# Reordering the first stage of a hybrid attention step: blank products, an earlier weight transfer, and 256-token products that lag by three

## The chip, the cores and the metric

One NeuronCore of a Trainium2 chip runs the whole program. The metric is the time of one execution on the device, in microseconds (us); before the change its median over three runs is 698.73 us (698.7 to 698.9). The engines are named as in the profile: PE is the matrix engine (PEld its weight loads), DVE the vector engine, ACT the scalar engine, POOL the GpSimd engine, SP the engine that issues most of the transfers. Each engine works through its own instructions in the order in which they stand, and semaphores tie the engines together.

## The reference: what is computed

One layer of a diffusion backbone on 128 context tokens and 1024 latent tokens, 1024 channels, all in float32:

```python
shift, scale, gate = split(silu(cond) @ w_mod + b_mod, 3)      # cond: c_ctx for context, c for latent
h = rmsnorm(x, norm_gain) * (1 + scale) + shift
q_a, k_a, v_a, g_a, q_b, k_b, v_b, g_b = split(h @ w_in)       # two head groups, 8 heads of 64 each
# rms norm of q and k per head, rotary positions on latent tokens,
# group A: attention to all keys, group B: band of +-128 keys with a sink; both also to the context keys
x = x + gate * (concat(o_a * silu(g_a), o_b * silu(g_b)) @ w_out)
```

The outputs are the new x of both token sets and the context keys and values. Only the part up to `g_a = h @ w_in[:, g_a]` matters here, that is the modulation, the norm and the first projection.

## The kernel before

Tokens lie in nine tiles of 128: tile 0 is the context, tiles 1 to 8 the latent tokens. Channels lie in eight blocks of 128, counted by k or j. The first stage (lines 430 to 563) does this for every tile: load it (`load_x`, L387), square and sum it on ACT (`squares`, L392), turn the mean square into a factor on POOL (L394, L396), multiply the tile by it on DVE (`scaled`, L399), turn it on PE in eight 128x128 transposes (`turned_tile`, L409) and copy the result from the two banks to `xT`, one half on ACT and one on DVE (`keep`, L413).

Beside it, for each channel block j, 1 MB of modulation weights `wm[j]` is loaded (`load_wm`, L334, three buffers). Eight small PE products give the modulation rows (`modulate_rows`, L363), a copy and two PE transposes bring them into columns (`modulate`, L374 to L380), and `modulated` (L424 to L428) makes the modulated block `h` as a high part `h0` (ACT) and a low part `h1` (`hf` on DVE, then a difference on POOL). The weights of the gate projection arrive as eight blocks `rawga` of 256 KB (`W_GA.load`, L229, three buffers) and are split likewise into `whiga` (ACT, L241) and `wloga` (DVE, L243).

The loop `for j in range(1, KT + 2)` (L498) is what the rest of the text calls steps. Step j does the gate products of block j-1 for the first 512 tokens: four output chunks `pg_f` ("big", `first_gates`), each with three products of 128x512 (high by high, high by low, low by high: L270, L271, L266). In the same step stand the modulation of block j, which the next step's products need, and the turning of one more tile: tile 5 in step 1, tile 6 in step 2, tiles 7, 8, 0 in steps 3, 4, 5 (`rest`). The squares of tile 7, 8 or 0 are taken one step before it is turned. Twelve products of 128x256 for tokens 512 to 767 (`pg_s`, "small", `next_gates`) close each step from step 2 on, for block j-2. `warm(n)` issues n products of a zero tile ("blank products", L447) whose result nobody reads.

What sets the order: `in_order` (L100) ties the instructions of every engine to the order in which the Python code writes them, so no scheduler moves anything. All transfers of this stage but one are issued by SP, into one queue; a transfer is issued when its buffer is free, and those behind it wait for it.

Of the kernel before, what the change touches and what calls it, by code (L numbers as in the profile page):

```python
# [36 lines left out]
LAG = 3  # L37
LEAD = 4
# [22 lines left out]
WARM = (12, 4)  # L61
# [53 lines left out]
def hybrid_step(ctx, tc, x_prompt, x_sample, cache_k_a, cache_v_a, cache_k_b, cache_v_b,  # L115
# [31 lines left out]
    mm_tags = ["BAAB"]  # L147
# [173 lines left out]
    with tc.tile_pool(name="st", bufs=2, side="right") as st:  # L321
# [27 lines left out]
        def conditions():  # L349

            nc.vector.tensor_copy(colt, pcol)
            nc.vector.tensor_copy(sil32[:, :, 0:2], sil2)
            nc.vector.tensor_scalar(bsc1, colt[:, 32:40], 1.0, None, op0=ALU.add)
            nc.vector.tensor_copy(ident_r, ident)
            nc.gpsimd.tensor_scalar(diag, ident[0:4, 0:4], -1.0, None, op0=ALU.mult)
# [14 lines left out]
        def modulate(j):  # L370
            pm = pmod.pop(j)[:, 256:512]
            for s in range(2):
                cs = slice(P * s, P * s + P)
                nc.tensor.transpose(pm[:, cs], mrows[j][:, cs], ident)  # L374
            m4 = st.tile([P, 2, 2], F32, tag="m4", name=f"m4_{j}")
            nc.vector.tensor_reduce(m4, pm.rearrange("p (s g c) -> p s c g", s=2, c=32)[:, :, 0:2, :], axis=AX.X,
                                    op=ALU.add)
            nc.vector.tensor_scalar(a_mod[:, j, :], m4[:, 0], bsc1[:, j : j + 1], colt[:, 16 + j : 17 + j],
                                    op0=ALU.add, op1=ALU.mult)
            nc.vector.tensor_scalar(b_col[:, j, :], m4[:, 1], colt[:, 24 + j : 25 + j], None, op0=ALU.add)  # L380

        xn, rx, px = {}, {}, {}
        xT = st.tile([P, KT, TOK], F32, name="xT", bufs=1)

        def load_x(t):
            xn[t] = st.tile([P, D], F32, tag="xn", name=f"xn{t}", bufs=4)
            nc.sync.dma_start(xn[t], x_tile[t])  # L387

        def squares(t):
            sq = st.tile([P, D], BF16, tag="sq", name=f"sq{t}", bufs=1)  # L390
            ss = st.tile([P, 1], F32, tag="ss", name=f"ss{t}")
            nc.scalar.activation(sq, xn[t], AF.Square, accum_out=ss)  # L392
            ms = st.tile([P, 1], F32, tag="ms", name=f"msx{t}")
            nc.gpsimd.tensor_scalar(ms, ss, 1.0 / D, EPS, op0=ALU.mult, op1=ALU.add)  # L394
            rx[t] = st.tile([P, 1], F32, tag="rs", name=f"rsx{t}", bufs=4)
            nc.gpsimd.tensor_tensor(rx[t], ms, mhalf[:, 0:1], op=ALU.pow)  # L396
# [4 lines left out]
        def turned_tile(t, tags, between=None):  # L401

            for c in range(2):
                if c and between:
                    between()
                px[t, c] = bank(tags[c], f"px{t}_{c}")
                for i in range(4):
                    k = 4 * c + i
                    nc.tensor.transpose(px[t, c][:, P * i : P * i + P], xn[t][:, P * k : P * k + P], ident)  # L409

        def keep(t, c, copy):
            at = slice(P * place(t), P * place(t) + P)
            copy(xT[:, 4 * c : 4 * c + 4, at], px.pop((t, c)).rearrange("p (k n) -> p k n", n=P))  # L413
# [16 lines left out]
        for t in (1, 2, 3, 4):  # L430
            load_x(t)
        load_wm(0)
        W_GA.load()
        load_wm(1)
        load_x(5)
        load_x(6)
        W_GA.load()
        load_wm(2)
        W_GA.load()
        load_x(7)  # L440
        load_x(8)
# [24 lines left out]
        nc.tensor.transpose(pcol, crow, ident[0:48, 0:48])  # L466
        for t in (1, 2, 3, 4):
# [3 lines left out]
        for t, tags in ((1, "AB"), (2, "AB"), (3, "CC")):  # L471
            scaled(t)
            if t == 2:
                conditions()
            if t == 3:
                modulate_rows(0, 0)
            turned_tile(t, tags)
            if t > 1:
                for c in range(2):
                    keep(t - 1, c, copies[c])  # L480
        scaled(4)
        modulate_rows(0, 1)
        keep(3, 0, copies[0])
        W_GA.split(nc.gpsimd)
        turned_tile(4, "AB", lambda: modulate(0))
        keep(4, 0, copies[0])
        modulated(0, 1, 4, 0)
        keep(3, 1, copies[1])
        keep(4, 1, copies[1])
        load_wm(3)  # L490
        load_x(0)
        squares(5)
        warm(WARM[1])
        big = [bank("AABB"[ch], f"pg0_{ch}_f") for ch in range(4)]
# [3 lines left out]
        for j in range(1, KT + 2):  # L498
            big_on, small_on = j <= KT, 2 <= j
# [4 lines left out]
            if big_on:  # L504
# [4 lines left out]
            if j == 2:  # L509
                turned_tile(6, "CC")  # L510
                for c in range(2):
                    keep(6, c, copies[c])
                small = [bank("C", f"pg0_{ch}_s") for ch in (0, 2)]
                for k in range(2):
                    modulated(k, 5, 2, 0)
            if j < KT:
                modulate_rows(j)
                if j + 3 < KT:
                    load_wm(j + 3)
            if j == 1:  # L520
                scaled(5)
                squares(6)
# [4 lines left out]
            if big_on:  # L527
                first_gates(0, j - 1, 1)
                first_gates(1, j - 1, 1)
                first_gates(2, j - 1, 1 if j == KT else None)  # L530
            if j < KT:
                modulate(j)
                if j == 1:
                    W_GA.split()
                modulated(j, 1, 4, 0)
                if j == 1:
                    scaled(6)
            if big_on:
                first_gates(3, j - 1)
            if j == 1:  # L540
                turned_tile(5, "DE")
                for c in range(2):
                    keep(5, c, copies[c])
# [6 lines left out]
            for ch in range(4):  # L550
                if small_on:
                    next_gates(ch, j - 2)
# [912 lines left out]
```

## Time and profile before

| what | value |
|---|---|
| median of three runs | 698.73 us (698.7 to 698.9) |
| the profiled execution's own time | 698.91 us |
| its span, first to last instruction | 697.2 us |
| granted PE clock, mean | 0.999 |
| PE busy | 689.9 us, 99% of the span |
| first real product of step 1 | 14.90 us |
| steps 2, 3 and 4 begin on PE | 20.24, 27.22 and 33.83 us |

Times inside the span count from its first instruction. A row of the timeline gives the start, the length, the engine, the line and operation, output and inputs, shape, how many equal ones were merged, and in brackets the idle time before it with the engine that ended it. The table of stretches gives for each stretch the busy time of each engine with its number of instructions, the granted PE clock, the mean busy share of the 16 DMA engines and what they moved in GB/s. A row of the chain of waits is start, length and what ran or was waited for.

### The profile page before, as it was taken

How to read it: one execution, taken by the hardware profiler on the slowest of the kernel's cores; microseconds unless marked ns; L12 is line 12 of the kernel's file. 1: busy time of each engine (PE TensorE's matmuls, PEld its weight loads, DVE VectorE, ACT ScalarE, POOL GpSimd, SP SyncE). 2: the span in 40 equal slices, each digit the busy share in tenths (PEclk: the TensorE clock that was granted, in tenths of full speed). 3: DMA queues.
4: the chain of work that ended last, by engine and by line, in shares of the span. 5: the costliest groups of instructions: out<-in, count | busy, mean ns of one | idle time of the engine just before them, and what ended most of it. 6: DMA issues, size and time to landing. Idle time of an engine off the chain costs nothing.

```text
span 697.2 us, 10663 instructions
## 1 busy us (share of the span) xinstructions
PE 689.9 (99%) x3537; PEld 558.6 (80%) x3537; DVE 464.3 (67%) x1010; ACT 409.9 (59%) x845; POOL 340.3 (49%) x359
## 2 busy tenths in 40 slices
PE   8999999999999999999999999999999999999997
PEld 4778988878788889987878888788788888887876
DVE  4767258968778855757777577666775775675563
ACT  6646312412423423198787887787778778877770
POOL 4547033232223420269665745565566557556751
PEclk9999999999999999999999999999999999999999
DMA  9962283359444016433122121212221221212323
GB/s 345 412 216 90 77 304 77 91 145 276 109 105 122 18 59 209 132 102 99 49 78 83 46 84 54 91 39 76 69 84 36 80 75 47 84 53 91 100 75 122
DMA packets 53336, 78.51 MB, mean 113 GB/s; under 512 B 6952, under 2 KB 25496, under 8 KB 52384
## 3 DMA queue, kind: packets, MB, share of 16 engines
q1 hardware_dynamic: 45040, 65.86, 28.6%
q10 hardware_dynamic: 8240, 11.96, 6.4%
q8 instruction: 28, 0.46, 0.3%
q14 instruction: 28, 0.23, 0.1%
HBM read 58.63 MB, written 19.18 MB: 112 GB/s over the span
## 4 chain that ended last, share of the span: by engine, by line
PE 94%; DMA 2%; ACT 2%; DVE 1%; issue 0%; SPq 0%; POOL 0%; ACTq 0%
PE po L1311 14%; PE pv L1233 7%; PE pv L1230 7%; PE st L1209 5%; PE pmx L920 5%; PE pv L1232 5%; PE st L1210 5%; PE pq L256 5%; PE pq L258 5%; PE pq L257 5%; PE st L1204 4%; PE pg L266 3%; PE pg L270 3%; PE pg L271 3%; PE pk L257 2%; PE pk L258 2%
## 5 line engine op out<-in xcount | busy, mean ns | idle before, releaser
L1220 POOL TENSOR_TENSOR pl<-pe,ph 128x512 fp32r<-128x512 f32 x130 | 168.5, 1298 | 134.2 <-DVE nm L976 65.4
L921 DVE TENSOR_REDUCE mx<-pmx 128x1 f32<-128x384 f32 x192 | 101.2, 553 | 56.1 <-PE pmx L920 54.0
L1212 ACT ACTIVATE pe<-st 128x512 f32<-128x512 f32 x146 | 86.9, 595 | 28.3 <-PE st L1210 27.7
L1216 ACT CAST ph<-pe 128x512 fp32r<-128x512 f32 x146 | 90.7, 621 | 4.8
L1230 PE MATMUL pv<-ph,v_hi 128*128 128x512 f32 x208 | 82.3, 396 | 0.1
L1233 PE MATMUL pv<-pl,v_hi 128*128 128x512 f32 x208 | 82.1, 395 | 0.2 <-DVE pl L1206 0.2
L976 DVE CUSTOM_DVE_ANT_0 sn<-sn,mask,nsink 128x512 f32<-128x512 f32 (+1 forms) x64 | 46.3, 724 | 41.9 <-PE sn L973 40.5
L181 POOL TENSOR_TENSOR rs_q<-ms_q,mhalf 128x8 f32<-128x8 f32 x18 | 34.2, 1898 | 80.8 <-DVE ms_q L179 80.8
L1311 PE MATMUL po<-wo,ogh 128*128 128x512 f32 (+1 forms) x224 | 73.4, 388 | 0.0
L920 PE MATMUL pmx<-kha,qt 128*128 128x384 f32 x192 | 60.4, 362 | 0.0
L1209 PE MATMUL st<-qt,kha 128*128 128x512 f32 x144 | 57.9, 402 | 0.0
L1232 PE MATMUL pv<-ph,v_lo 128*64 128x512 f32 x146 | 57.6, 395 | 0.0
L1210 PE MATMUL st<-qb,kla 68*128 68x512 f32 x144 | 57.3, 398 | 0.0
L1233 PEld LDWEIGHTS pv<-pl,v_hi 128*128 128x128 f32 x208 | 39.0, 188 | 17.5 <-DVE pl L1206 0.6
L962 ACT ACTIVATE pen<-sn,nm 128x512 f32<-128x512 f32 (+2 forms) x72 | 45.0, 627 | 6.0 <-DVE nm L976 2.7
L1205 ACT CAST ph<-st 128x512 fp32r<-128x512 f32 x62 | 36.4, 587 | 20.1 <-PE st L1204 18.8
L1311 PEld LDWEIGHTS po<-wo,ogh 128*128 128x128 f32 x224 | 41.0, 188 | 6.4 <-ACT ogh L1273 0.3
L1230 PEld LDWEIGHTS pv<-ph,v_hi 128*128 128x128 f32 x208 | 39.2, 189 | 7.6 <-issue 0.6
L1206 DVE TENSOR_TENSOR pl<-st,ph 128x512 fp32r<-128x512 f32 x62 | 42.5, 686 | 2.8 <-ACT ph L1205 2.3
L679 ACT CAST qo0q<-ptq 128x512 fp32r<-128x512 f32 x18 | 10.6, 587 | 57.4 <-PE ptq L676 57.4
L1311 PE MATMUL po<-wo,ogl 128*128 128x512 f32 (+1 forms) x112 | 43.6, 389 | 0.0
L920 PEld LDWEIGHTS pmx<-kha,qt 128*128 128x128 f32 x192 | 35.4, 190 | 4.5
(238 smaller groups left out, 1702.3 us busy)
## 6 DMA issues: line engine op xcount, KB each, us to landing
qt<-qd SPq DMA_DIRECT2D x36, 256.0 KB, 3.2
wm<-in_w_mod_ss_dram SPq DMA_DIRECT2D x7, 1024.0 KB, 11.1
qd<-qo0q ACTq DMA_DIRECT2D x36, 128.0 KB, 2.4
qd<-qo1q ACTq DMA_DIRECT2D x36, 128.0 KB, 2.4
sgl<-gd SPq DMA_DIRECT2D x35, 128.0 KB, 2.6
out_dram<-yt SPq DMA_DIRECT2D x17, 256.0 KB, 2.1
xn<-in_x_sample_dram SPq DMA_DIRECT2D x8, 512.0 KB, 6.1
wg<-in_w_mod_g_dram SPq DMA_DIRECT2D x4, 1024.0 KB, 8.5
```

The costliest lines, as they stand in the source:

```text
L257: nc.tensor.matmul(out, h_at(0, i, k, tok), w.lo[k], start=False, stop=False)
L920: nc.tensor.matmul(pm[:, 0:384], lhs, kha[:, g, 3 * b : 3 * b + 3, :], start=True, stop=True)
L921: nc.vector.tensor_reduce(mx[:, h, b : b + 1], pm[:, 0:384], axis=AX.X, op=ALU.max)
L1209: nc.tensor.matmul(s, kh, qtile[i], start=True, stop=False)
L1210: nc.tensor.matmul(s, kl, qbtile[i], start=False, stop=True)
L1212: nc.scalar.activation(pe, s, AF.Exp)
L1216: nc.scalar.copy(ph, pe)
L1220: nc.gpsimd.tensor_tensor(pl, pe, ph, op=ALU.subtract)
L1230: nc.tensor.matmul(pv, two, ph, start=(b == 0), stop=False)
L1232: nc.tensor.matmul(pv[0:64, :], vl, ph, start=False, stop=False)
L1233: nc.tensor.matmul(pv, two, pl, start=False, stop=last)
L1311: nc.tensor.matmul(po[n, q.start], a, wo_parts[KT * n + k][lo][:, q], start=(k == KS[0] and p == 0), stop=(k == KS[-1] and p == 2))
```

## The change

Five things move, all in the first stage.

- Blank products: sixteen become 25. Five new ones stand behind the transpose of the conditions, two before tile 2's transposes and two before tile 3's.
- The head: the four tiles' squares come first on ACT; tile 4 is scaled straight after tile 3 on DVE but for one copy; the eight modulation products of block 0 run in one go. Small preparations go from DVE to ACT and POOL, and for blocks 0 and 1 the shift column (`b_col`) goes to ACT. For tiles 1 to 6 the mean square needs no step on POOL any more: the square is scaled on ACT, and a 1025th element holds the constant.
- Transfers: the fourth modulation weights `wm3` are asked for before tiles 7, 8 and 0. Tile 6 goes behind the second gate weights.
- Steps 1 and 2: step 1 takes its products of three chunks high part first; its DVE split of the second gate weights stands ahead of the modulation's reduction; tile 6 is turned at the end of step 2 and not in its middle.
- The small products lag by three steps and not two, so that the loop has one step more; the banks of the big outputs alternate (ABAB).

On SP's queue, before (the x tiles are `xn`, the modulation weights `wm`, the gate weights `rawga`):

```order
L387 DMA xn5_190<-in_x_sample_dram 128x1024
L387 DMA xn6_192<-in_x_sample_dram 128x1024
L229 DMA rawga_1_194<-in_w_in_dram 128x512
L334 DMA wm2_196<-in_w_mod_ss_dram 128x2048
L229 DMA rawga_2_198<-in_w_in_dram 128x512
L387 DMA xn7_200<-in_x_sample_dram 128x1024
L387 DMA xn8_202<-in_x_sample_dram 128x1024
L229 DMA rawga_3_307<-in_w_in_dram 128x512
L334 DMA wm3_333<-in_w_mod_ss_dram 128x2048
```

and with the change:

```order
L392 DMA xn5_194<-in_x_sample_dram 128x1024
L230 DMA rawga_1_196<-in_w_in_dram 128x512
L392 DMA xn6_198<-in_x_sample_dram 128x1024
L335 DMA wm2_200<-in_w_mod_ss_dram 128x2048
L230 DMA rawga_2_202<-in_w_in_dram 128x512
L335 DMA wm3_204<-in_w_mod_ss_dram 128x2048
L230 DMA rawga_3_316<-in_w_in_dram 128x512
L392 DMA xn7_342<-in_x_sample_dram 128x1024
```

Up to `rawga_2` the same bytes are asked for; behind it tile 7 (`xn7`) came next, and now `wm3` and `rawga_3` stand ahead of it.

On ACT, from the cast of the third gate weights in step 2 to the first products' operand of step 3 (`sq7` is the square of tile 7, `h0_0_2` the high part of block 2 for 512 tokens, `mrows2` the copy of block 2's modulation rows), before:

```order
L241 CAST whiga_2_415<-rawga_2_198 128x512
L413 COPY xT_174<-px6_0_425 128x4x128
L424 ACTIVATE h0_1_0_132<-xT_174,b_col_150,a_mod_149 128x256 x2
L368 COPY mrows2_456<-pm2_447 128x256
L392 ACTIVATE sq7_460,ss7_461<-xn7_200 128x1024
L424 ACTIVATE h0_0_2_118<-xT_174,b_col_150,a_mod_149 128x512
```

and with the change:

```order
L242 CAST whiga_2_419<-rawga_2_202 128x512
L368 COPY mrows2_438<-pm2_429 128x256
L401 ACTIVATE sq7_445,ms7_446<-xn7_342 128x1024
L433 ACTIVATE h0_0_2_118<-xT_174,b_col_150,a_mod_149 128x512
L422 COPY xT_174<-px6_0_469 128x4x128
L433 ACTIVATE h0_1_0_132<-xT_174,b_col_150,a_mod_149 128x256 x2
```

The square of tile 7 still stands directly ahead of `h0_0_2`; tile 6's copy and the 256-token operands went behind them.

On DVE in step 1, before:

```order
L368 COPY mrows1_366<-pm1_357 128x256
L399 TENSOR_SCALAR xn5_190<-xn5_190,rsx5_342 128x1024
L376 TENSOR_REDUCE m4_1_385<-pm1_357 128x4
L378 TENSOR_SCALAR a_mod_149<-m4_1_385,bsc1_170,colt_163 128x2
L380 TENSOR_SCALAR b_col_150<-m4_1_385,colt_163 128x2
L243 TENSOR_TENSOR wloga_1_390<-rawga_1_194,whiga_1_389 128x512
```

and with the change:

```order
L368 COPY mrows1_373<-pm1_364 128x256
L408 TENSOR_SCALAR xn5_194<-xn5_194,rsx5_347 128x1024
L244 TENSOR_TENSOR wloga_1_381<-rawga_1_196,whiga_1_380 128x512
L376 TENSOR_REDUCE m4_1_391<-pm1_364 128x4
L378 TENSOR_SCALAR a_mod_149<-m4_1_391,bsc1_170,colt_163 128x2
```

The split of the second gate weights moved ahead of the reduction, and the shift column left DVE.

The diff, cut to its core:

```diff
+LEADING = (1, 2, 3, 4, 5, 6)
-WARM = (12, 4)
+WARM = (12, 5, 2, 2, 4)
...
-            nc.vector.tensor_scalar(b_col[:, j, :], m4[:, 1], colt[:, 24 + j : 25 + j], None, op0=ALU.add)
+            bias = colt[:, 24 + j : 25 + j]
+            if j < 2:
+                nc.scalar.activation(b_col[:, j, :], m4[:, 1], AF.Identity, bias=bias)
+            else:
+                nc.vector.tensor_scalar(b_col[:, j, :], m4[:, 1], bias, None, op0=ALU.add)
...
         def squares(t):
-            sq = st.tile([P, D], BF16, tag="sq", name=f"sq{t}", bufs=1)
-            ss = st.tile([P, 1], F32, tag="ss", name=f"ss{t}")
-            nc.scalar.activation(sq, xn[t], AF.Square, accum_out=ss)
-            ms = st.tile([P, 1], F32, tag="ms", name=f"msx{t}")
-            nc.gpsimd.tensor_scalar(ms, ss, 1.0 / D, EPS, op0=ALU.mult, op1=ALU.add)
+            n = D + (t in LEADING)
+            sq = st.tile([P, D + 1], BF16, tag="sq", name=f"sq{t}", bufs=1)
+            ms = st.tile([P, 1], F32, tag="ms", name=f"ms{t}")
+            nc.scalar.activation(sq[:, 0:n], xe[t][:, 0:n], AF.Square, scale=D ** -0.5, accum_out=ms)
+            if t not in LEADING:
+                nc.gpsimd.tensor_scalar(ms, ms, EPS, None, op0=ALU.add)
...
         load_wm(1)
         load_x(5)
+        W_GA.load()
         load_x(6)
-        W_GA.load()
         load_wm(2)
         W_GA.load()
-        load_x(7)
-        load_x(8)
+        load_wm(3)
...
+        scaled(1)
+        turned_tile(1, "AB")
+        scaled(2)
+        nc.vector.tensor_copy(sil32[:, :, 0:2], sil2)
+        warm(WARM[2])
+        turned_tile(2, "AB")
+        scaled(3)
+        warm(WARM[3])
+        turned_tile(3, "CC")
+        for t in (1, 2, 3):
+            keep(t, 0, copies[0])
+        keep(1, 1, copies[1])
         scaled(4)
-        modulate_rows(0, 1)
-        keep(3, 0, copies[0])
+        keep(2, 1, copies[1])
+        keep(3, 1, copies[0])
+        modulate_rows(0)
...
-        load_wm(3)
-        load_x(0)
+        load_x(7)
         squares(5)
...
+        late = {1: 8, 2: 0}
-        for j in range(1, KT + 2):
-            big_on, small_on = j <= KT, 2 <= j
+        for j in range(1, KT + 3):
+            big_on, small_on = j <= KT, 3 <= j
...
-            if j == 2:
-                turned_tile(6, "CC")
...
             if j < KT:
                 modulate_rows(j)
                 if j + 3 < KT:
                     load_wm(j + 3)
+                if j in late:
+                    load_x(late[j])
...
-            if j == 1:
-                turned_tile(5, "DE")
+            if j in (1, 2):
+                turned_tile(4 + j, ("CC", "DE")[j - 1])
...
                 if small_on:
-                    next_gates(ch, j - 2)
+                    next_gates(ch, j - 3)
```

More of the change, by code (lines that the diff above doesn't have):

```diff
@@ L146, in hybrid_step @@
     turn = {"mm": 0, "tr": 0}
[L147 removed]
+    mm_tags = ["BABA"]
     def bank(tag, name):
@@ L349, in conditions @@
         def conditions():
[L351 to L354, printed above, removed]
+            nc.scalar.copy(colt, pcol)
+            nc.gpsimd.tensor_scalar(bsc1, colt[:, 32:40], 1.0, None, op0=ALU.add)
+            nc.gpsimd.tensor_copy(ident_r, ident)
             nc.gpsimd.tensor_scalar(diag, ident[0:4, 0:4], -1.0, None, op0=ALU.mult)
@@ L403, in turned_tile, with keep @@
             for c in range(2):
-                if c and between:
-                    between()
                 px[t, c] = bank(tags[c], f"px{t}_{c}")
                 for i in range(4):
+                    if c and i == 2 and between:
+                        between()
                     k = 4 * c + i
                     nc.tensor.transpose(px[t, c][:, P * i : P * i + P], xn[t][:, P * k : P * k + P], ident)
-        def keep(t, c, copy):
+        def keep(t, c, copy, a=0, b=4):
             at = slice(P * place(t), P * place(t) + P)
-            copy(xT[:, 4 * c : 4 * c + 4, at], px.pop((t, c)).rearrange("p (k n) -> p k n", n=P))
+            copy(xT[:, 4 * c + a : 4 * c + b, at], px[t, c].rearrange("p (k n) -> p k n", n=P)[:, a:b])
         def modulated(j, t0, n, cond):
@@ L431, in hybrid_step @@
             load_x(t)
+            padded(t, nc.vector)
         load_wm(0)
@@ L503, in hybrid_step @@
                 put_gates(big[0], 0, 0, slice(0, 512))
-            if big_on:
+            if j == 1:
+                for part in (W_GA.hi, W_GA.lo):
+                    for ch in range(3):
+                        nc.tensor.matmul(big[ch], part[0][:, P * ch : P * ch + P], h_at(0, 0, 0, slice(0, 512)),
+                                         start=(part is W_GA.hi), stop=False)
+            elif big_on:
                 first_gates(0, j - 1, 0)
@@ L508, in hybrid_step @@
                     first_gates(2, j - 1, 0)
-            if j == 2:
-                turned_tile(6, "CC")
-                for c in range(2):
-                    keep(6, c, copies[c])
+            if j == 3:
                 small = [bank("C", f"pg0_{ch}_s") for ch in (0, 2)]
-                for k in range(2):
-                    modulated(k, 5, 2, 0)
             if j < KT:
@@ L519, in hybrid_step @@
                     load_wm(j + 3)
+                if j in late:
+                    load_x(late[j])
+            if j in (1, 2):
+                scaled(4 + j)
             if j == 1:
-                scaled(5)
-                squares(6)
+                W_GA.split()
             if j in rest:
@@ L529, in hybrid_step @@
                 first_gates(1, j - 1, 1)
-                first_gates(2, j - 1, 1 if j == KT else None)
+                first_gates(2, j - 1, 1 if j in (1, KT) else None)
             if j < KT:
                 modulate(j)
-                if j == 1:
-                    W_GA.split()
                 modulated(j, 1, 4, 0)
                 if j == 1:
-                    scaled(6)
+                    squares(6)
             if big_on:
                 first_gates(3, j - 1)
-            if j == 1:
-                turned_tile(5, "DE")
+            if j in (1, 2):
+                turned_tile(4 + j, ("CC", "DE")[j - 1])
                 for c in range(2):
-                    keep(5, c, copies[c])
+                    keep(4 + j, c, copies[c])
+            if j == 2:
+                for k in range(2):
+                    modulated(k, 5, 2, 0)
             if j in rest:
```

29 lines of the change are left out of this document (13 added, 16 removed).

## The prediction

> **What bounds the kernel now.** I read the page first (span, busy shares, the chain that ended last), then PE's own waits over the whole run, then the table of stretches, and then the timeline of each engine where the change acts.
>
> ```profile
> span 697.2 us, 10663 instructions
> PE 689.9 (99%) x3537; PEld 558.6 (80%) x3537; DVE 464.3 (67%) x1010; ACT 409.9 (59%) x845; POOL 340.3 (49%) x359
> PE 94%; DMA 2%; ACT 2%; DVE 1%; issue 0%; SPq 0%; POOL 0%; ACTq 0%
> ...
> PE px L409 <- DVE xn L399: 1.2, 2, 0.8
> PE idle L447 <- DVE mhalf L170: 1.0, 1, 1.0
> PE pm L363 <- DMA wm<-in_w_mod_ss_dram: 0.2, 1, 0.2
> PE sn L972 <- ACT pen L962: 0.2, 1, 0.2
> ```
>
> PE bounds the whole run, and its waits, all in the head but for single ones of 0.2 us, make some 3 us. So two things follow. There is little to win: the change reorders the first 60 us and removes no PE work. And whatever PE newly waits there comes out at the end unchanged, because nothing later has slack on PE to give it back. The 2% of DMA in the chain say where to look for a new wait.
>
> ```profile
> core 0: us, PE busy (x) PEld busy (x) DVE busy (x) ACT busy (x) POOL busy (x), PEclk, DMA share, GB/s
> 15.00:20.00 5.00, 5.00 (x38) 3.52 (x38) 3.75 (x10) 3.44 (x6) 2.95 (x5) 1.00 1.02 410
> 20.00:25.00 5.00, 4.87 (x38) 3.08 (x37) 3.59 (x7) 3.36 (x8) 1.98 (x2) 1.00 1.04 415
> ```
>
> From 15 to 25 us the DMA engines are full (share 1.00 and over) at 410 to 415 GB/s. In this stretch it is the place in SP's queue that sets when a transfer lands, and a transfer that goes ahead of another delays it by its bytes.
>
> **The change part by part.** The steps on PE, as they are:
>
> ```profile
> 14.90 0.50 PE L270 MATMUL pg_f<-h,whiga 128*128 128x512 f32 x1 [0.18 <-ACT h L424]
> 20.24 0.50 PE L270 MATMUL pg_f<-h,whiga 128*128 128x512 f32 x1
> 24.28 0.40 PE L266 MATMUL pg_f<-h,whiga 128*128 128x512 f32 x1
> 24.81 0.44 PE L374 MATMUL pm<-ident,mrows 128*128 128x128 f32 x2
> 25.78 0.28 PE L270 MATMUL pg_s<-h,whiga 128*128 128x256 f32 x1
> 27.22 0.50 PE L270 MATMUL pg_f<-h,whiga 128*128 128x512 f32 x1
> 31.52 1.04 PE L409 MATMUL px<-ident,xn 128*128 128x128 f32 x8
> ...
> 25.48 0.23 PE pg_f L271
> ```
>
> The last row is the chain's: behind a product of 512 columns the next one starts after 0.23 us.
>
> *The head, and the blank products.* Twelve blank products took 5.30 us at the start and four took 1.03 us later (rows below). The nine new ones so cost 2.3 us, or 4.0 us where PE still runs at the first pace; they fill holes of 0.8 us and less (the waits above), so tile 1's transposes come later by up to 1.5 us.
>
> ```profile
> 1.03 5.30 PE L447 MATMUL idle<-blank 128*128 128x512 bf16 x12 [1.03 <-DVE mhalf L170]
> 13.70 1.03 PE L447 MATMUL idle<-blank 128*128 128x512 bf16 x4
> 10.21 0.64 PE L363 MATMUL pm<-wm,sil 128*32 128x256 f32 x8 [0.20 <-DMA wm<-in_w_mod_ss_dram]
> 13.94 0.22 DVE L380 TENSOR_SCALAR b_col<-m,colt 128x2 f32<-128x2 f32 x1
> ```
>
> The first half of wm0 lands at 10.2, its second half (0.52 MB at 410 GB/s) so at 11.5; that is the cover of the blanks, since tiles 1 to 3 are turned by about 11. Block 0's eight products then end near 12.0, 0.35 us earlier than now. The shift column beside and not behind the scale column saves some 0.2. The first product comes at about 14.4 instead of 14.90 (bounds: 14.2, and 15.4 where the blanks run at the first pace).
>
> *Step 2's start swallows that.* It hangs on tile 5's landing, which does not move:
>
> ```profile
> 15.87 1.06 ACT L392 ACTIVATE sq<-xn 128x1024 bf16<-128x1024 f32 x1 [1.02 <-DMA xn<-in_x_sample_dram]
> 17.38 0.56 POOL L396 TENSOR_TENSOR rsx<-msx,mhalf 128x1 f32<-128x1 f32 x1
> 17.97 0.75 DVE L399 TENSOR_SCALAR xn<-xn,rsx 128x1024 f32<-128x1024 f32 x1 [0.38 <-POOL rsx L396]
> 18.71 0.17 DVE L376 TENSOR_REDUCE m<-pm 128x4 f32<-128x16 f32 x1
> 19.25 0.68 DVE L243 TENSOR_TENSOR wloga<-rawga,whiga 128x512 fp32r<-128x512 f32 x1
> 19.37 0.81 ACT L424 ACTIVATE h<-xT,b_col,a_mod 128x512 fp32r<-128x512 f32 x1 [0.53 <-DVE b_col L380]
> ```
>
> Without the POOL step ahead of the factor, tile 5's scaling starts 0.28 earlier, at 17.7, and ends at 18.45. Now the split of the weights (0.68, of which 0.6 shows) comes ahead of the reduction, which so starts at 19.0 instead of 18.71. The shift column on ACT saves about 0.1 of the 0.66 between reduction and h. The operand starts near 19.55, ends at 20.35, and PE begins step 2 at 20.4: 0.15 later than now. Gain of the head: nothing.
>
> *Step 2 itself.* Tile 6's transposes only change places. PE's wait of 0.30 (24.28 + 0.23 to 24.81) goes, because ACT no longer does two 256-token operands ahead of the rows' copy. The twelve small products (25.78 to 27.22, 1.44 us) move to the loop's end. PE is through with step 2 at 20.4 + 5.54 - 0.30 = 25.65. Measured by equal work this stands against 25.78 now: even.
>
> *The fourth modulation weights.* They arrive 4 us earlier, but PE waited for modulation weights once in the whole run, 0.2 us, for wm0. That wins nothing. What they delay is tile 7:
>
> ```profile
> 11.37 10.88 DMA rawga<-in_w_in_dram
> 22.27 0.62 ACT L241 CAST whiga<-rawga 128x512 fp32r<-128x512 f32 x1 [1.61 <-DMA rawga<-in_w_in_dram]
> 24.66 1.06 ACT L392 ACTIVATE sq<-xn 128x1024 bf16<-128x1024 f32 x1
> 25.62 0.19 ACT L392 ACTIVATION_READ_ACCUMULATOR sq<-xn 128x1 f32 x1
> ```
>
> The third gate weights land at 11.37 + 10.88 = 22.25, and up to them the same bytes are asked for in both kernels. Then come wm3 (1.05 MB), the fourth gate weights (0.26) and tile 7 (0.52): 1.83 MB at 410 to 415 GB/s, 4.45 us. Tile 7 lands at 26.7. Now its square starts at 24.66 and waits for no transfer; it will wait until 26.7, and on ACT block 2's high part is queued right behind it, then tile 6's copy, the 256-token operands and the fourth cast. A square holds ACT for 1.05 us before the next starts (24.66 to 25.62, plus most of the 0.19), so h starts at 27.8, ends 0.81 later at 28.6, and PE begins step 3 at 28.65. It was ready at 25.65: a wait of 3.0 us. Against equal work in the kernel before (27.22 - 1.44 = 25.78) the loss is **2.87 us**.
>
> *What is late next.* PE turns tile 7 4.30 us into step 3 (31.52 - 27.22), so at 32.95. Its scaling on DVE stands behind work that waited for ACT:
>
> ```profile
> 20.09 0.57 ACT L413 COPY xT<-px 128x512 f32<-128x512 f32 x1
> 45.98 1.48 ACT L424 ACTIVATE h<-xT,b_col,a_mod 128x256 fp32r<-128x256 f32 x3
> 28.20 0.88 DVE L243 TENSOR_TENSOR wloga<-rawga,whiga 128x512 fp32r<-128x512 f32 x1 [0.89 <-ACT whiga L241]
> 29.00 1.22 DVE L399 TENSOR_SCALAR xn<-xn,rsx 128x1024 f32<-128x1024 f32 x1
> ```
>
> ACT after h (28.55): tile 6's copy 0.5, three operands 1.48, a cast 0.6, to 31.15. Then DVE: the split 0.7 to 0.9 beside a busy POOL, tile 7's scaling 0.75 alone to 1.22 beside POOL, done between 32.6 and 33.3, later still if POOL's differences of the 256-token operands drag too. PE's wait is 0 to 0.7; I take **0.4**, nearest to the rows beside a busy POOL. From step 4 on tile 8 (26.7 + 3.8 = 30.5) and tile 0 are in time, and I count the lag, the renamed banks and the extra step at nothing: same products, operands long there (if the lag hid nothing, at most the 1.44 us of one round would show).
>
> The sum: 698.91 (the profiled execution: span 697.2 and 1.7 around it) + 2.87 + 0.4 = 702.2. That execution is 0.2 above the median, so the forecast for the median is **702.0 us**, slower by 0.47%.
>
> *Bounds.* Tile 5's square shows it landed at 15.8; from there to 22.25 the queue moved tile 6, the second and third gate weights and wm2, 2.10 MB, which take 5.1 us at the full rate. The row is 1.35 late, so one transfer had a straggler. If that does not recur, tile 7 lands at 25.35 and the loss is 1.5 + 0 to 0.7: 700.2. If a second one comes, 703.6.
>
> **The rivals.** *A, the PE clock falls in the new wait.* The first twelve blank products show a slow pace (0.44 us each against 0.26 later), while the clock column reads 1.00. If a 3 us hole sent PE back there, the 12 products' difference, 5.30 - 12 x 0.26 = 2.2 us, is the price: 704.2. Against it: holes of 0.8 us did nothing, but a hole of 3 us is not in this trace. The Trainium skill, "TensorE: Matmul & The Clock Gate" (section "Why this matters for your kernels"), advises against PE gaps of over about 3 us, while its Part 1 ("What's actually happening") puts the drop at an idle window of about 3.4 us. By the first the clock would fall here, by the second it would not; no row of this trace decides. Chance 0.06.
>
> *B, tile 7 is there in time.* If the queue served its transfers side by side, or faster, tile 7 could land before 24.0, so that its square ends as block 2's scale and shift columns are done (near 25.1). Then no wait is left, and what stays is the 0.30 of step 2's wait and a little of the head: 698.3 to 698.7. For it, the page's times to landing:
>
> ```profile
> wm<-in_w_mod_ss_dram SPq DMA_DIRECT2D x7, 1024.0 KB, 11.1
> xn<-in_x_sample_dram SPq DMA_DIRECT2D x8, 512.0 KB, 6.1
> ```
>
> A tile takes 6.1 us in the median, and it is now asked for well before 20 us (its buffer is free and the fourth gate weights' too, once block 0's split is done). Against it: the engines are full, and 1.83 MB do not go through in the 1.75 us from 22.25 to 24.0. Chance 0.09, of which 0.03 that it ends faster by over 0.2%.
>
> *C, only part shows.* Tile 7's landing falls between 24.0 and 25.2, with no second wait: 0.2 to 1.4 us lost, 699.4. It needs the straggler gone and a higher rate too. Chance 0.05.
>
> **How the numbers follow.** The forecast (wait for tile 7, with or without the wait at its transposes) has 0.80, and its own range is 700.2 to 703.6. The range for 8 in 10 is the same; it leaves A, B and C out, which hold 0.20. About 0.2% (1.4 us) is what a measurement of this kernel can tell from no change. Slower by more: the forecast and A, with a little of C, 0.87. Within: most of B and of C, 0.10. Faster: 0.03.
>
> **What would show it.** In the profile of the changed kernel: ACT's square of tile 7 waits some 3.5 us for the transfer of xn and starts near 26.7; PE's first product of step 3 waits some 3 us for ACT's h and starts near 28.65; step 2 starts near 20.4 although step 1 starts near 14.4; the wait for the rows' copy at 24.81 is gone; tile 7's transposes wait under 0.7 us for DVE's scaling; products after the wait still follow each other at 0.23 us. It is wrong if tile 7's square finds its data there, if PE fills the wait with other work, or if a later stage gives the 3 us back.

## The result, and the profile after

| | before | changed |
|---|---|---|
| median | 698.77 us (6 runs, 698.57 to 699.13) | 703.55 us (6 runs, 702.94 to 705.18) |
| profiled execution: time, span | 698.91, 697.2 | 705.18, 703.5 |
| ratio | | 1.0069 [1.0056, 1.0082] |

The change makes the kernel 0.69% slower. The forecast was 702.0 us with a range of 700.2 to 703.6, and slower at 0.87. The direction and the mechanism came out as forecast. The size was 1.5 us short at the median, and the execution that was profiled lies 3 us above the forecast of 702.2 made on the old profile.

PE's waits in the changed kernel; the columns are what PE ran and the line, the engine and product that ended the wait, then the sum, the number and the longest wait in us:

```profile
span 703.5 us, 10690 instructions
PE pg_f L271 <- ACT h L433: 3.3, 2, 2.9
PE pg_f L524 <- ACT h L433: 0.7, 1, 0.7
PE px L418 <- DVE xn L408: 0.5, 1, 0.5
```

One long wait is new: 2.9 us for ACT's high part, ahead of step 3 (the group's other 0.4 us stand ahead of step 2). ACT's rows around it, from the timeline of the changed kernel (start, length, engine, line and operation, and in brackets the idle time before it):

```profile
22.40 0.62 ACT L242 CAST whiga<-rawga 128x512 fp32r<-128x512 f32 x1 [0.38 <-DMA rawga<-in_w_in_dram]
26.94 1.06 ACT L401 ACTIVATE sq<-xn 128x1024 bf16<-128x1024 f32 x1 [3.65 <-DMA xn<-in_x_sample_dram]
28.00 0.80 ACT L433 ACTIVATE h<-xT,b_col,a_mod 128x512 fp32r<-128x512 f32 x1
```

The third gate weights land at 22.40, tile 7 at 26.94; ACT idles 3.65 us at tile 7's square, and block 2's high part, queued behind it, begins only at 28.00. And PE in the same stretch:

```profile
14.78 0.96 PE L524 MATMUL pg_f<-h,whiga 128*128 128x512 f32 x3 [0.66 <-ACT h L433]
20.56 0.50 PE L271 MATMUL pg_f<-h,whiga 128*128 128x512 f32 x1 [0.44 <-ACT h L433]
24.93 1.03 PE L418 MATMUL px<-ident,xn 128*128 128x128 f32 x8
28.85 0.80 PE L271 MATMUL pg_f<-h,whiga 128*128 128x512 f32 x1 [2.88 <-ACT h L433]
29.44 0.63 PE L272 MATMUL pg_f<-h,wloga 128*128 128x512 f32 x1
29.87 0.63 PE L271 MATMUL pg_f<-h,whiga 128*128 128x512 f32 x1
35.99 1.03 PE L418 MATMUL px<-ident,xn 128*128 128x128 f32 x8
```

Behind the wait products start 0.43 us apart (29.44 to 29.87), where they were 0.23 apart before. The table of stretches gives the reason (the column before the last two is the granted PE clock):

```profile
25.00:30.00 5.00, 2.12 (x12) 1.69 (x11) 2.07 (x5) 3.02 (x6) 1.74 (x3) 0.83 1.02 407
30.00:35.00 5.00, 5.00 (x24) 2.53 (x23) 3.81 (x5) 2.81 (x6) 3.52 (x6) 0.50 1.01 369
```

The clock fell to half in the 5 us after 30.

Step starts on PE tell where the time came from. A kernel whose small products lag by three steps has done one round of them less (1.44 us) at the start of step 3 and later, so the row "before, less one round" is what it compares with.

| first product of step | 1 | 2 | 3 | 4 | 8 |
|---|---|---|---|---|---|
| before | 14.90 | 20.24 | 27.22 | 33.83 | 58.11 |
| before, less one round | | | 25.78 | 32.39 | 56.67 |
| changed | 14.78 | 20.56 | 28.85 | 38.29 | 62.57 |

Step 2 is 0.3 us late, step 3 is 3.07 late, step 4 is 5.90 late, and step 8 still 5.90. The span grew by 6.3. So 5.6 of the 6.3 us are lost between 25 and 38 us, 2.8 in the wait and another 2.8 at the half clock in step 3, and no later stage gives any of it back.

### The profile page after: what moved, and what is told of

Its sections match the earlier page's. It is cut to its first block, busy times and chain, and to the rows that moved or that the text cites. A ratio compares the mean times of both kernels' runs of the same rounds, so it can differ in the third digit from the quotient of the medians.

```text
span 703.5 us, 10690 instructions
## 1 busy us (share of the span) xinstructions
PE 693.2 (99%) x3546; PEld 560.6 (80%) x3546; DVE 464.3 (66%) x1008; ACT 410.7 (58%) x850; POOL 338.5 (48%) x357
## 4 chain that ended last, share of the span: by engine, by line
PE 94%; DMA 2%; ACT 1%; DVE 1%; issue 0%; POOL 0%; ACTq 0%; DVEq 0%
PE po L1332 14%; PE pv L1254 7%; PE pv L1251 7%; PE st L1230 5%; PE pmx L941 5%; PE pv L1253 5%; PE st L1231 5%; PE pq L259 5%; PE pq L257 5%; PE pq L258 5%; PE st L1225 4%; PE pg L267 3%; PE pg L271 3%; PE pg L272 3%; PE pk L258 2%; PE pk L259 2%
```

## The experiments

Eleven kernels ran, in three groups. Each group shares its runs of the kernel before, whose medians were 699.23 us (first four), 699.17 (next four) and 699.42 (last three). "+1.94" means that many us above the median of the kernel before in the same group. The start of step 1 scatters between executions by more than a microsecond with the same head (14.57 to 15.79), as the first tiles land at different times (ACT begins the third tile's square between 6.91 and 8.09 us); so I compare differences inside one profile, and the medians.

**Tile 7 first.** The changed kernel with the places of the two transfers exchanged.

```diff
-        load_wm(3)
+        load_x(7)
...
-        load_x(7)
+        load_wm(3)
         squares(5)
```

> The change with tile 7 asked for ahead of the fourth modulation weights, all else as in the change. Theory 1 (tile 7's late landing makes the wait ahead of step 3, and the wait lets the PE clock fall): tile 7's square finds its data near 23.6 us, PE begins step 3 near 26.0 us, the granted clock stays at 1.00 from 25 to 35 us, and the time is that of the kernel before within 0.7 us, 698.2 to 699.5. Theory 2 (the loss comes from the rest of the change: lag of three, blank products, DVE order of step 1): the time stays above 701. New cost that is possible: up to 0.5 us of waiting for the fourth modulation weights in step 3, which land near 26.8.

Measured: 701.17 us (700.49 to 701.85), +1.94, ratio 1.0028 [1.0018, 1.0038]. The wait ahead of step 3 is gone (step 3 starts at 26.35) and the clock is 1.00 throughout. That is what theory 1 said of the wait and the clock, and 2.8 of the 4.8 us lost go with it. But 1.94 us stay with tile 7 in time, above the 698.2 to 699.5 of theory 1 and just inside theory 2's "above 701": neither holds in full. ACT's high part of block 2 and the first product of step 3 in its profile:

```profile
25.49 0.81 ACT L433 ACTIVATE h<-xT,b_col,a_mod 128x512 fp32r<-128x512 f32 x1 [0.41 <-DVE b_col L384]
26.35 0.51 PE L271 MATMUL pg_f<-h,whiga 128*128 128x512 f32 x1
```

The small products lag by three steps here too, and PE still does not wait ahead of step 3.

**Order alone.** The kernel before with the changed order of transfers and nothing else.

```diff
-        load_x(7)
-        load_x(8)
+        load_wm(3)
...
-        load_wm(3)
-        load_x(0)
+        load_x(7)
...
+                if j in late:
+                    load_x(late[j])
```

> The kernel before with only the order of the transfers changed (fourth modulation weights ahead of tiles 7, 8, 0). Theory 1: tile 7 lands at 26.9 as in the changed kernel and block 2's operand is done at 28.75, but here PE has the twelve 256-token products to do meanwhile (until 27.2), so it waits only 1.6 us; that is too short for the clock to fall: 700.2 to 700.9, clock 1.00 all along. If the clock fell as easily here: 701.5 to 703. Theory 2: 698.5 to 699.

Measured: 700.53 us (700.31 to 701.22), +1.30, ratio 1.0020 [1.0011, 1.0029]: the time is as expected, the wait a little shorter than the 1.6 us expected. ACT's and PE's rows in its profile:

```profile
26.72 1.06 ACT L392 ACTIVATE sq<-xn 128x1024 bf16<-128x1024 f32 x1 [2.07 <-DMA xn<-in_x_sample_dram]
28.62 0.50 PE L270 MATMUL pg_f<-h,whiga 128*128 128x512 f32 x1 [1.12 <-ACT h L424]
```

Tile 7 is as late as in the changed kernel (26.72 against 26.94), but PE waits 1.12 us and not 2.88. The twelve small products at the end of step 2, which the lag of two leaves there, fill 1.44 us of the hole.

**The square behind the operands.** The changed kernel, its transfers as they are, but tile 7's square issued behind the operands of step 2.

```diff
-            if j + 1 in rest:
+            if j + 1 in rest and j > 2:
                 squares(rest[j + 1])
...
                 modulated(j, 5, 2, 0)
+            if j == 2:
+                squares(7)
```

> The change with tile 7's square moved on ACT behind block 2's operand, tile 6's copy and the 256-token operands of step 2; transfers as in the change. Theory 1 says that it is the place in ACT's queue that hands the late landing on to PE: step 3 begins near 26.0 us, the clock stays, and what is left is 0.5 to 1.0 us in step 3, where the rows' copy and tile 7's scaling now come late: 699.0 to 700.0. If PE needed tile 7 itself that early, the time would stay above 701.5.

Measured: 701.68 us (700.82 to 702.27), +2.45, ratio 1.0035 [1.0022, 1.0047]. The wait ahead of step 3 is gone here too (step 3 at 26.81), although the transfers stand as in the change: what cost PE the time was that block 2's high part stood behind the square on ACT. (When tile 7 lands is not to be seen here: the square begins at 28.75 and waits for nothing.) But the time did not come down to the 699 to 700 expected, and by the number alone the rival's "above 701.5" is met; what stays is the residue of the first experiment, and more, since the late square now makes tile 7's scaling late: at its transposes PE waits, by the groups of waits,

```profile
PE px L418 <- DVE m L376: 1.0, 1, 1.0
PE pm L374 <- ACT mrows L368: 0.3, 1, 0.3
```

and the second row is the rows' copy, which the square now delays on ACT.

**Blank products in the wait.** The changed kernel with thirteen blank products at the end of step 2.

```diff
             if j == 2:
+                warm(13, "C")
                 for k in range(2):
```

> The change with 13 blank products (2.8 us at 0.216 each) at the end of step 2, in a bank that is free there, so that PE is busy through the wait; every wait stays. Theory 1 with the clock: step 3 begins at 28.85 as in the changed kernel, its products follow each other at 0.23 us and not 0.43, the granted clock is 1.00 from 25 to 35 us, and tile 7's transposes now wait 0.3 to 0.7 us for DVE, which the slow clock covered; the time is 701.7 to 702.6, below the changed kernel's median of 703.55, with less spread. If the clock has no share in the time: no change, 703 to 704.

Measured: 703.13 us (702.95 to 703.43), +3.90, ratio 1.0057 [1.0045, 1.0070].

```profile
24.76 1.03 PE L418 MATMUL px<-ident,xn 128*128 128x128 f32 x8
25.63 2.97 PE L456 MATMUL idle<-blank 128*128 128x512 bf16 x13
28.68 0.50 PE L271 MATMUL pg_f<-h,whiga 128*128 128x512 f32 x1
33.80 1.09 PE L418 MATMUL px<-ident,xn 128*128 128x128 f32 x8 [0.66 <-DVE m L376]
```

DVE in the same profile, from the 256-token operands to tile 7's scaling:

```profile
29.14 2.23 DVE L436 TENSOR_SCALAR hf<-xT,a_mod,b_col 128x256 f32<-128x256 f32 x3 [2.62 <-ACT xT L422]
31.29 1.23 DVE L244 TENSOR_TENSOR wloga<-rawga,whiga 128x512 fp32r<-128x512 f32 x1
32.44 1.23 DVE L408 TENSOR_SCALAR xn<-xn,rsx 128x1024 f32<-128x1024 f32 x1
33.59 0.16 DVE L376 TENSOR_REDUCE m<-pm 128x4 f32<-128x16 f32 x1
```

By its number alone the run is a miss: 703.13 lies above the 701.7 to 702.6 expected and in the range given for a clock without a share in the time, 703 to 704. The profile shows the rest as the theory had it. Filled with work that nobody reads, the hole costs the same, products stand 0.23 us apart behind it, and the clock stays at 1.00 in every stretch. Step 3 is 2.90 us late (28.68 against 25.78), step 4 3.77 late. Step 3 takes 7.48 us here, 0.87 more than before (6.61), and that is the wait at tile 7's transposes, whose scaling on DVE ends only at 33.67 (PE's row names the reduction right behind it, and counts 0.66 us from the end of the last product's row, which at 0.39 to 0.40 us is 0.16 longer than the 0.23 after which the next could start). In the profile of the change the half clock hid it: there PE came to them late enough. Its profiled execution took 702.95 us, as much as the two quickest runs of the changed kernel (702.94, 702.95, both at a mean clock of 0.999). Three others took 703.43 to 703.71 at 0.997, the profiled one 705.18 at 0.995. So the fall of the clock costs 2.2 us in the profiled execution and nothing to be seen in the two quickest. What it costs at the median is not shown: the two kernels' medians differ by 0.42 us, and by 0.9 when each is taken against its own runs of the kernel before, but the intervals overlap; and a mean clock of 0.997 does not tell where the clock fell (the kernel before has runs of 698.93 and 698.97 us at 0.997, below its median).

**The operands spread.** "Tile 7 first", and the 256-token operands made one block per step, two steps later than in the change.

```diff
-            if j == 2:
-                for k in range(2):
-                    modulated(k, 5, 2, 0)
...
-            if 1 < j < KT:
-                modulated(j, 5, 2, 0)
+            if 1 < j <= KT + 1:
+                modulated(j - 2, 5, 2, 0)
```

> Edit: the changed kernel with tile 7 ahead of the fourth modulation weights (as in e1), and the 256-token operands made one block per step, block j-2 in step j, two steps later than in the change (three blocks at the end of step 2 become one), so that they lag with the products that read them. Theory of the bunch: in e1 the three operands (1.95 us on DVE at the end of step 2, beside POOL's differences) push the split of the weights, tile 7's scaling and the reduction back, and PE waits 0.64 us at tile 7's transposes (30.67 to 31.31); spread out this wait goes, and 0.65 of e1's 1.94 us goes with it: 1.3 us above the kernel before, 700.2 to 700.9 at a before of 699.23. Rival (the residue of e1 comes from the head and from step 1, and a wait taken away in step 3 comes back in a later step): 700.9 to 701.5, as e1.

Measured: 702.40 us (701.41 to 702.44), +3.23, ratio 1.0042 [1.0030, 1.0055]: worse than either expectation. The first two fences below are DVE and PE of "tile 7 first"; the third is PE of this kernel, a row of its waits and two of its timeline.

```profile
26.93 1.95 DVE L436 TENSOR_SCALAR hf<-xT,a_mod,b_col 128x256 f32<-128x256 f32 x3
28.94 1.09 DVE L244 TENSOR_TENSOR wloga<-rawga,whiga 128x512 fp32r<-128x512 f32 x1
29.95 1.22 DVE L408 TENSOR_SCALAR xn<-xn,rsx 128x1024 f32<-128x1024 f32 x1
```

```profile
31.31 1.09 PE L418 MATMUL px<-ident,xn 128*128 128x128 f32 x8 [0.47 <-DVE m L376]
```

```profile
PE pg_s L267 <- POOL h L437: 1.8, 2, 1.4
30.90 1.04 PE L418 MATMUL px<-ident,xn 128*128 128x128 f32 x8
65.64 0.39 PE L267 MATMUL pg_s<-h,whiga 128*128 128x256 f32 x1 [1.36 <-POOL h L437]
```

Spreading does what it was to do: the transposes of tile 7 no longer wait. But the last blocks' operands are then made too late for the loop's tail, where POOL has other differences to do, and PE waits 1.8 us at 62 to 66 us. The edit was a bad test of a right idea.

**The split behind the reduction.** "Tile 7 first", and step 1's DVE split of the second gate weights back behind the reduction.

```diff
-            if j == 1:
-                W_GA.split()
...
                 modulate(j)
+                if j == 1:
+                    W_GA.split()
                 modulated(j, 1, 4, 0)
```

> Edit: e1, and in step 1 DVE's split of the second gate weights goes back behind the reduction and the scale column, as in the kernel before. Theory: in e1 step 2 starts 0.71 us later than before, of which 0.44 us is PE's wait for ACT's high part, and that hangs on the reduction, which waits 0.6 us for the split. Without the split ahead of it the wait goes: 0.4 us less than e1, 700.4 to 701.0 at a before of 699.23. Rival (the wait hangs on tile 5's scaling or on the shift column on ACT, or the split's low part is then late for step 2's second product): 701.0 to 701.4.

Measured: 700.77 us (700.15 to 701.30), +1.60, ratio 1.0022 [1.0013, 1.0030], inside the expectation of 700.4 to 701.0. PE's wait ahead of step 2, which was to go, falls from 0.44 us to 0.25:

```profile
21.39 0.50 PE L271 MATMUL pg_f<-h,whiga 128*128 128x512 f32 x1 [0.25 <-ACT h L433]
```

The intervals of this kernel and of "tile 7 first" overlap, so 0.3 us is what the medians say, not what they prove.

**Spread and behind.** Both edits together.

> Edit: both edits of e5 and e6 on top of e1. Theory: the two add up, 1.05 us less than e1, and what is left, some 0.9 us above the kernel before, is the later start of step 1 and step 1's own product order: 699.7 to 700.5 at a before of 699.23. If both are the whole residue, level with the kernel before (699.0 to 699.6). Rival (neither is the cause): 700.9 to 701.5.

Measured: 702.25 us (701.65 to 702.48), +3.08, ratio 1.0040 [1.0026, 1.0053], above all three of its ranges: the same 1.8 us of waits for POOL stand in the tail. It tells nothing on the sum of the two.

**Half the dose.** The changed kernel with tile 7 behind the fourth modulation weights but ahead of the fourth gate weights, 0.26 MB less in front of it.

```diff
         load_wm(3)
+        load_x(7)
...
-        load_x(7)
         squares(5)
```

> Edit: the change, but tile 7 asked for directly behind the fourth modulation weights and ahead of the fourth gate weights (0.26 MB), so tile 7 has 0.26 MB less ahead of it. Theory (the place in the queue times the rate sets the wait): tile 7's square starts 0.63 us sooner (26.3 instead of 26.94), PE's wait ahead of step 3 is 2.25 us instead of 2.88, and the time 0.6 us under that of the change without a fall of the clock (3.9 us above the kernel before): 3.3 us above the kernel before, 702.2 to 702.9 at a before of 699.23, without the spread up to 2.2 us that the change shows, if a hole of 2.25 us leaves the clock alone. Rival (the queue serves its transfers side by side, so that the order matters little): 703.0 to 703.8.

Measured: 702.68 us (702.12 to 704.02), +3.51, ratio 1.0053 [1.0041, 1.0066]; the median is inside the 702.2 to 702.9 expected, the spread is not. ACT, PE and a stretch of its profile:

```profile
23.10 0.62 ACT L242 CAST whiga<-rawga 128x512 fp32r<-128x512 f32 x1 [0.38 <-DMA rawga<-in_w_in_dram]
26.96 1.06 ACT L401 ACTIVATE sq<-xn 128x1024 bf16<-128x1024 f32 x1 [2.97 <-DMA xn<-in_x_sample_dram]
28.86 0.50 PE L271 MATMUL pg_f<-h,whiga 128*128 128x512 f32 x1 [2.18 <-ACT h L433]
30.00:35.00 5.00, 5.00 (x30) 3.23 (x30) 4.41 (x8) 2.85 (x7) 4.09 (x6) 0.66 1.00 372
```

All starts 0.7 us later in this execution, so the landing of the third gate weights is the mark. From there to tile 7 it takes 3.86 us, against 4.54 in the change (22.40 to 26.94): 0.68 less for 0.26 MB, which at 410 GB/s is 0.64. PE's wait is 2.18 us, 2.25 were expected. So the bytes ahead in the queue, over the rate, set the wait. The clock fell here too, behind a hole of 2.18 us.

**Spread, but caught up.** "The split behind the reduction", and the 256-token operands spread over steps 2 to 5 and back in their old places from step 6 on.

```diff
-            if j == 2:
-                for k in range(2):
-                    modulated(k, 5, 2, 0)
...
-            if 1 < j < KT:
-                modulated(j, 5, 2, 0)
+            for k in {2: (0,), 3: (1,), 4: (2, 3), 5: (4, 5), 6: (6,), 7: (7,)}.get(j, ()):
+                modulated(k, 5, 2, 0)
```

> Edit: the changed kernel with tile 7 ahead of the fourth modulation weights, step 1's split of the weights behind the reduction (as in e6), and the 256-token operands spread over the steps but caught up before the loop's tail: block 0 in step 2, 1 in step 3, 2 and 3 in step 4, 4 and 5 in step 5, 6 and 7 in their own steps. Theory of the bunch: e5 lost 1.8 us at the tail alone (PE's waits for POOL's last low parts); with the tail as in the change this is gone, PE's wait of 0.6 to 0.7 us at tile 7's transposes stays away as it did in e5, and the time is e6's 1.6 us above the kernel before less 0.65: 0.95 us above it, 699.9 to 700.5 at a before of 699.2. Rival (the wait only moves, to step 4 or 5, where two operands now stand together): as e6, 700.5 to 701.2.

Measured: 699.93 us (699.25 to 700.51), +0.51, ratio 1.0004 [0.9995, 1.0013]: inside its expectation and no longer to be told from the kernel before. It is 1.1 us under "the split behind the reduction", where the three operands still stand in a bunch; the wait that was to go accounts for 0.65 of that, and no run assigns the rest (the two intervals just touch). PE passes from its product of step 3 to tile 7's transposes without a wait, and the tail's waits are gone:

```profile
30.74 0.40 PE L267 MATMUL pg_f<-h,whiga 128*128 128x512 f32 x1
30.98 1.04 PE L418 MATMUL px<-ident,xn 128*128 128x128 f32 x8
```

**The head alone.** The kernel before with the changed head: blank products, tile 4 scaled early (the four squares, which the list of changes names too, stand first on ACT in both kernels), the padded square, conditions and shift column off DVE.

```diff
-WARM = (12, 4)
+WARM = (12, 5, 2, 2, 4)
...
-            nc.vector.tensor_copy(colt, pcol)
+            nc.scalar.copy(colt, pcol)
...
+            if j < 2:
+                nc.scalar.activation(b_col[:, j, :], m4[:, 1], AF.Identity, bias=bias)
```

> Edit: the kernel before with the head of the change alone (blank products, squares first, tile 4 scaled early, conditions on ACT and POOL, the padded square, the shift column on ACT); transfers, steps 1 and 2 and the lag as before. Prediction's theory (the head's gain is nothing, step 2 hangs on tile 5): 698.8 to 699.6 at a before of 699.2. Rival H (the residue of e1 and e6 sits in the head, step 1 begins some 0.3 to 0.9 us later than in the kernel before): 699.8 to 700.4.

Measured: 699.74 us (699.36 to 700.25), +0.32, ratio 1.0004 [0.9995, 1.0013]: no change that can be told, a little on the slow side, and between the two ranges (698.8 to 699.6, and 699.8 to 700.4). In the changed kernel's profile the first operand comes only 0.1 us earlier than in the kernel before:

```profile
13.37 0.67 DVE L378 TENSOR_SCALAR a_mod<-m,bsc,colt 128x2 f32<-128x2 f32 x1
14.14 0.41 DVE L435 TENSOR_SCALAR h<-xT,a_mod,b_col 128x256 fp32r<-128x256 f32 x1
```

and in the kernel before

```profile
13.67 0.35 DVE L378 TENSOR_SCALAR a_mod<-m,bsc,colt 128x2 f32<-128x2 f32 x1
14.26 0.41 DVE L426 TENSOR_SCALAR h<-xT,a_mod,b_col 128x256 fp32r<-128x256 f32 x1
```

The scale column takes 0.67 us, against 0.35. So the time that the shift column's move to ACT was to save is not there. In the ten profiles with the changed head it takes 0.53 to 0.68 us, in the three with the old one 0.29, 0.35 and 0.61; what makes it longer was not tried.

**The lag alone.** The kernel before with the small products lagging by three steps.

```diff
-        for j in range(1, KT + 2):
-            big_on, small_on = j <= KT, 2 <= j
+        for j in range(1, KT + 3):
+            big_on, small_on = j <= KT, 3 <= j
...
-                    next_gates(ch, j - 2)
+                    next_gates(ch, j - 3)
```

> Edit: the kernel before with the 256-token products lagging by three steps instead of two, and nothing else. Prediction's theory (the lag costs nothing, since operands are long there): 698.9 to 699.6 at a before of 699.2. Rival L (the twelve products that closed step 2 covered the time in which ACT and DVE make step 3's operand, so that their 1.44 us come out as a wait ahead of step 3): up to 1.44 us later, 699.8 to 700.7, and step 3 then waits for ACT's high part.

Measured: 700.72 us (700.16 to 701.27), +1.30, ratio 1.0016 [1.0007, 1.0026]. In the kernel before the prediction's theory falls and the rival holds, at the upper end of its range (699.8 to 700.7); ACT's high part first, then PE:

```profile
26.65 1.31 ACT L424 ACTIVATE h<-xT,b_col,a_mod 128x512 fp32r<-128x512 f32 x2 [0.55 <-DVE b_col L380]
25.99 0.40 PE L266 MATMUL pg_f<-h,whiga 128*128 128x512 f32 x1
27.52 0.49 PE L270 MATMUL pg_f<-h,whiga 128*128 128x512 f32 x1 [1.13 <-ACT h L424]
```

Without the twelve small products at the end of step 2, PE stands 1.13 us before step 3 and waits for block 2's high part, which was never late before because those products covered it. The cover was just enough: in the kernel before that part begins at 26.35 on ACT and step 3 at 27.22, 0.87 us later, as here (26.65 and 27.52).

## Why the prediction was right, and where it was wrong

| step of the prediction | foretold | measured |
|---|---|---|
| step 1 begins | 14.4 (14.2 to 15.4) | 14.78 |
| step 2 begins | 20.4 | 20.56 |
| wait for the rows' copy in step 2 | gone | gone |
| tile 7's square, its wait | 26.7, 3.5 | 26.94, 3.65 |
| step 3 begins, the wait before it | 28.65, 3.0 | 28.85, 2.88 |
| products after the wait | 0.23 us apart | 0.43 in the profiled execution |
| wait at tile 7's transposes | 0.4 (0 to 0.7) | 0 at the half clock, 0.8 without the fall |
| the lag | nothing, or up to 1.44 | 1.30 in the kernel before; no wait ahead of step 3 in "tile 7 first" |

*The transfer behind which ACT waits.* The chain of the forecast is confirmed link by link: the queue's bytes at 410 GB/s (half the dose took 0.68 us off, 0.64 by the bytes), the square that waits, the high part behind it (the square moved away: the wait is gone with the transfers as in the change), and PE (tile 7 first: the wait is gone).

*"I count the lag ... at nothing".* For the kernel before this is wrong: the lag alone costs 1.30 us there. In the changed kernel it holds, as far as the runs show, while tile 7 is in time. "Tile 7 first" keeps the lag, and PE does not wait ahead of step 3: block 2's high part begins at 25.49, and the transposes of tile 6, which the change moved to the end of step 2 (from 25.25 on in that profile), stand where the small products stood. "Spread, but caught up" keeps the lag too and is level with the kernel before. What the lag takes away is 1.44 us of cover for a late tile 7: with a lag of two PE waits 1.12 us for it ("order alone"), here 2.88, and the comparison by equal work had that in the 2.87. How the 2.87 divide between transfer and lag no run says, since the change with a lag of two did not run; with the transfers put back, 2.84 of the 4.78 us go.

*The wait at tile 7's transposes, mis-sized.* The term was 0.4 and measured 0.8 where the clock held (step 3 longer by 0.87). Its cause was named rightly (work that waited on DVE beside POOL), but too short rows were taken: the split took 1.23 us, where 0.7 to 0.9 were put, and the scaling 1.23, the top of its bounds, so DVE was through at 33.67 and not between 32.6 and 33.3. It is also not only "what is late next": with tile 7 in time it stays, as PE's 0.6 us, because the change itself bunches three operands where two and one were. Spreading them out took 1.1 us off.

*Rival A, at 0.06, happened.* The clock fell in the hole. Its price of 2.2 us, from the first twelve blank products, fits: the profiled execution lies 2.2 above the kernel with blanks in the hole (705.18 against 702.95). In part that is chance: the half clock made step 3 2.8 us longer, and about 2 are left only because it hid the 0.87 at the transposes. What the row of small holes could not tell is that its price differs between executions of one kernel, from nothing to be seen to 2.2 us; the profile is the end of that scale. Of the Trainium skill's two figures, the advice in "TensorE: Matmul & The Clock Gate" ("Why this matters for your kernels") against gaps of over some 3 us was nearer than a drop only at an idle window of 3.4 us (Part 1), and 2.18 us were already enough, under both.

*The sum, once more.* "Blanks in the wait" is the forecast's own case, the clock not fallen: 3.77 us at step 4 in its profile and +3.90 at the median, where the forecast had 2.87 + 0.4 = 3.27. Of the 0.63 between, 0.47 stand at tile 7's transposes, and 0.16 no run assigns. The changed kernel itself is at +4.78; the 0.9 above the blanks fit the clock, but the intervals overlap. Rivals B and C are out: tile 7 was nowhere near 24.0.

*Luck in the range.* The median, 703.55, lies 0.05 us inside the range's upper end. That end was set for a second late transfer, and none came (tile 7's square begins at 26.94, for 26.7 foretold). The room was used up by the transposes and by the clock, which the range was said to leave out. The lower end, 700.2, took away the 1.35 us by which the third gate weights came later than their bytes ask for, as the accident of one execution. It was not that: from the start of tile 5's square to the cast of these weights the eight profiles in which ACT waits for them show 5.9 to 6.6 us, for the 5.1 worked out. Direction and mechanism were no luck; that the number is inside is.

*What is left over.* With tile 7 in time, the split behind and the operands spread, the changed kernel is level with the one before, with its lag of three and its head. The residue of 1.94 is, by the medians, 0.3 for the split, 1.1 for the bunch and 0.5 that cannot be told from nothing. No version ran faster than the kernel before.

## What to carry to other kernels

Small work that fills a gap is cover: before a batch of products is moved to a later place, look what becomes ready only while it runs, since the wait appears where the batch stood and the batch's time at the end. A transfer moved ahead in a full queue costs the one behind it its bytes over the rate, and the price is paid by whatever stands behind the first reader on that reader's engine, so moving that reader back is an alternative to moving the transfer. Where two edits bear on the same wait, test them one by one and also inside the change: the lag alone made a wait in the old order of step 2 and none in the new one while the tile was in time.

## What the runs showed of the hardware that was not expected

The half clock comes in pieces of one length. From the granted clock of the 5 us stretches, the time at half speed is twice what is missing: in "half the dose" (0.66 in one stretch) 2 x 0.34 x 5 = 3.4 us; in the changed kernel (0.83, 0.50, and 0.99 from 35 to 40) 1.7 + 5.0 + 0.1 = 6.8 us, twice that. In "order alone" the clock fell in the head, after 1.79 us in which PE waited for tile 1 (from 5.4 to 7.2), which the changed head fills with blank products:

```profile
PE px L409 <- DVE xn L399: 1.8, 1, 1.8
5.00:10.00 5.00, 3.21 (x17) 2.89 (x16) 2.86 (x8) 4.37 (x10) 2.64 (x7) 0.74 1.01 351
10.00:15.00 5.00, 5.00 (x42) 2.98 (x40) 3.10 (x8) 2.65 (x6) 2.51 (x4) 0.92 1.02 423
```

That is 2 x (0.26 + 0.08) x 5 = 3.4 us again. It fits a clock that is decided anew every 3.4 us, and the Trainium skill ("TensorE: Matmul & The Clock Gate", Part 1) describes such a free-running window; but the holes of 1.79, 2.18 and 2.88 us were all shorter than a window, and holes of up to 1.36 us (the tail of "the operands spread") left the clock at 1.00. Nor does the clock fall with the hole: in "half the dose" PE is at work again from 28.86, its first products start 0.23 us apart, and in stretches of 1 us the clock reads 1.00 from 29 to 30, then 0.64, 0.50, 0.50 and 0.65, so it fell near 30.3, 1.4 us after the hole. So a window need not be idle from end to end for the clock to fall; where the bound lies between, and how it hangs on the place of the hole in the window, no run here shows. In the head the fall cost nothing to be seen: that execution was the quickest of its kernel (700.31 us), since PE waits for the tiles there anyway.
